# A two-group layer on one core: where the third group's second feed-forward product stands

## The chip, the cores and the metric

One core of a Trainium2 chip runs the kernel. The metric is the device time of one execution in microseconds (us), of which lower is better. The engines are TensorE (PE: matmuls; PEld: its weight loads), VectorE (DVE), ScalarE (ACT), GpSimd (POOL) and SyncE (SP), which issues most DMAs. Each engine executes its own instructions in a fixed order.

## The reference, cut to what matters

```python
u  = x*(1+sc1) + sh1                       # z = u @ w_in; then RG-LRU branch A and band attention B
x1 = LN(alpha*x + (1+g1) * ((sigmoid(ga)*A + sigmoid(gb)*B) @ w_out))
u2 = x1*(1+sc2) + sh2
y  = LN(alpha*x1 + (1+g2) * (relu(u2 @ w_up + b_up)**2 @ w_down + b_down))
```

The model width is 1024, the hidden width of the last line 4096, and there are 1024 prompt and 64 sample tokens. All is float32. The change concerns the last line only.

## The kernel before, in words

Tokens lie along the free dimension in three groups of 384, 384 and 320 (the third holds the 64 sample tokens). Every fp32 product is made of three matmuls, `mm3` (lines 108 to 111): each operand is split into a rounded high part (ScalarE, a copy, line 96 or 102) and the remainder as low part (VectorE, a subtraction, line 97 or 103).

**The up product** (`u2 @ w_up`) has 32 feature blocks, taken as 16 pairs p = 0 to 15. For pairs 3 to 15 the groups 1 and 2 together go through a seven-product scheme (`strassen`, from the weight sums that `wops` forms on GpSimd, and operands T1 to T4): accumulators `xu`, `zu`, `yu`, 12 matmuls to a product, the results `c` passed through relu and square (lines 608, 609) and written to DRAM (`hs_d`, seven operands for each of four chunks c). The third group goes through a plain product `up_g2` (accumulators `ug`, results `cg`, DRAM `hg_d`), 24 matmuls to a block. For pairs below `LATE` = 11 it stands inside its pair; for pairs 11 to 15 it comes after all pairs, from weights that are loaded and split a second time.

**The down product** follows in three steps: for each of four chunks seven operands `op` are loaded from `hs_d` and split (`op_split`; two raw buffers `opr`, seven split ones `oph`/`opl`), then four seven-product blocks (`xd`, `zd`, `yd`) are added into `facc` by VectorE (line 840). Then the third group's product `dg` runs in 2 x 4 x 4 blocks of 24 matmuls (half r of the output, chunk, output block b), for which `hg` is loaded in 16 pieces, and between these blocks `final(g, i)` normalizes the six finished token tiles of groups 1 and 2 (transposes `yt` on TensorE, statistics and a product on VectorE, an addition on GpSimd at line 872, copies on ScalarE). The last three tiles, `final(2)`, are the tail.

Before the up product, `early(i)` puts up products of pairs 0 and 1 between the steps of the first normalization (`ln1`), whose transposes `nt` give the operands `u2h`, `u2l`. The order of the instructions on each engine is set by a scheduler in the framework, which simulates the program; the order of the source is its input, `issue_after` its constraint. Weights go through three raw buffers `wraw` and three of each split part.

Of the kernel before, what the change touches and what calls it, by code (L numbers as in the profile page):

```python
# [48 lines left out]
def body(nc, tc, a):  # L49
    V, S, G, TE, SY = nc.vector, nc.scalar, nc.gpsimd, nc.tensor, nc.sync  # L50
    with ExitStack() as es:
# [552 lines left out]
        def up_w(f):  # L604
            return wsplit(a["w_up"][f], f"u{f}")
# [32 lines left out]
        def fblocks(p):  # L638
            c, i = divmod(p, 4)
            return 8 * c + i, 8 * c + 4 + i  # L640
# [11 lines left out]
        def early(i):  # L652
            for f in (ef[0:2], (), ef[2:4], ())[i] if i < 4 else ():
                wt[f] = up_w(f)
                up_mm(f, wt[f], 0)
            for f in ((), ef[0:2], (), ef[2:4])[i] if i < 4 else ():
                up_mm(f, wt[f], 1)

        ln1(2, rTs[2], early)
# [48 lines left out]
        def wops(src1, src2, nm, full):  # L708

            raw = []  # L710
            for b, src in enumerate((src1, src2)):
                r = wp.tile([P, NB, P], F32, tag="wraw", name=f"wr_{nm}{b}")
                SY.dma_start(r, src)
                raw.append(r)
            ra, rb = raw
            sr, sums = [], []
            for b in range(2):
                sr.append(spool[0].tile([P, NB, P], F32, tag="sraw", bufs=2, name=f"sr_{nm}{b}"))
                sums.append([spool[0].tile([P, NB, P], R32, tag=t, bufs=2, name=f"{t}_{nm}{b}") for t in ("shi", "slo")])
            h = slice(0, 4), slice(4, 8)  # L720
            s1, s2, s3, s4 = sr[0][:, h[1], :], sr[0][:, h[0], :], sr[1][:, h[0], :], sr[1][:, h[1], :]
            wa = [wp.tile([P, NB, P], R32, tag=t, name=f"{t}_{nm}0") for t in ("whi", "wlo")]
            split(*wa, ra)
            G.tensor_tensor(s1, rb[:, h[0], :], rb[:, h[1], :], op=ALU.add)
            G.tensor_tensor(s2, s1, ra[:, h[0], :], op=ALU.subtract)
            split(*sums[0], sr[0])
            G.tensor_tensor(s3, ra[:, h[0], :], rb[:, h[0], :], op=ALU.subtract)
            G.tensor_tensor(s4, ra[:, h[1], :], s2, op=ALU.subtract)
            split(*sums[1], sr[1])
            wb = [wp.tile([P, NB, P], R32, tag=t, name=f"{t}_{nm}1") for t in ("whi", "wlo")]  # L730
            if full:
                split(*wb, rb)
            else:
                split(wb[0][:, h[1], :], wb[1][:, h[1], :], rb[:, h[1], :])

            def half(t, k):
                return t[0][:, h[k], :], t[1][:, h[k], :]

            ops = [half(wa, 0), half(wa, 1), half(sums[0], 0), half(sums[0], 1), half(sums[1], 0), half(sums[1], 1), half(wb, 1)]
            return ops, wa, wb  # L740
# [13 lines left out]
        def up_g2(p, wa, wb):  # L754
            for b, (wt, f) in enumerate(zip((wa, wb), fblocks(p))):
                ps = acc(f"ug{p}_{b}")
                for kb in range(NB):
                    mm3(ps[:, :TW2], wt[0][:, kb, :], wt[1][:, kb, :], u2h[2][:, kb, :], u2l[2][:, kb, :], kb == 0, kb == NB - 1)
                c = fp.tile([P, TW2], F32, tag="cg", bufs=2, name=f"cg{p}_{b}")
                relu2(c, ps[:, :TW2], f)  # L760
                put_g2(p, b, c)

        PLAIN, LATE = 3, 11

        def up_pair(p):
            f1, f2 = fblocks(p)
# [36 lines left out]

        for p in range(2, 16):
            up_pair(p)
        for p in range(LATE, 16):
            up_g2(p, *(up_w(f) for f in fblocks(p)))
        up_es.close()


# [5 lines left out]
        def op_split(src, nm):  # L816
            hl = [hp.tile(list(src.shape), R32, tag=t, bufs=7, name=f"{t}{nm}") for t in ("oph", "opl")]
            split(*hl, src)
            return hl

        for c in range(4):
            ops = []
            for k in range(7):
                o = hp.tile([P, 4, GW], F32, tag="opr", bufs=2, name=f"op{c}_{k}")
                last = SY.dma_start(o, hs_d[c, k]).ins
                ops.append(op_split(o, f"{c}_{k}"))
            if c == 0:
                with tc.issue_after(last):
                    for fb in range(NB):
                        facc[fb] = hp.tile([P, TS2], F32, tag=f"facc{fb}", name=f"facc{fb}")  # L830
                        SY.dma_start(facc[fb], facc_d[:, fb, 0:TS2])
            for j in range(4):
                w, wa, wb = wops(a["w_down"][c, 2 * j], a["w_down"][c, 2 * j + 1], f"d{c}_{j}", False)

                def after(k, ps):

                    for b, g in {0: [(0, 0)], 1: [(0, 0)], 2: [(0, 1)], 3: [(1, 1)], 4: [(1, 1)], 5: [(0, 1)], 6: [(1, 0)]}[k]:
                        fb = 2 * j + b
                        fc = facc[fb][:, GW * g:GW * g + GW]
                        V.scalar_tensor_tensor(fc, ps, ada[:, G2, fb, 0:1], fc, op0=ALU.mult, op1=ALU.add)  # L840

                strassen(w, ops, f"d{c}_{j}", after)

        with tc.issue_after(last):
            fg = actb.tile([P, NB, TW2], F32, tag="act", bufs=2, name="fg")
            SY.dma_start(fg, facc_d[:, :, TS2:T])
            lgb = actb.tile([P, 2, D], F32, tag="act", bufs=2, name="lgb")
            lg, lb = lgb[:, 0, :], lgb[:, 1, :]
            SY.dma_start(lg, a["ln2"][0].partition_broadcast(P))
            SY.dma_start(lb, a["ln2"][1].partition_broadcast(P))  # L850
        hg = {}

        def facc_of(g, fb, c, cw):
            return fg[:, fb, c:c + cw] if g == 2 else facc[fb][:, GW * g + c:GW * g + c + cw]
# [32 lines left out]
            for c in todo:  # L887
                finish(*c)

        for r in range(2):  # L890
            ps = [acc(f"dg{4 * r + b}") for b in range(4)]
            for c in range(4):
                for h in range(2):
                    o = hp.tile([P, 4, TW2], F32, tag="opr", bufs=2, name=f"hg{r}_{c}_{h}")
                    SY.dma_start(o, hg_d[:, 8 * c + 4 * h:8 * c + 4 * h + 4, :])
                    hg[h] = op_split(o, f"g{r}_{c}_{h}")
                for b in range(4):
                    wh, wl = wsplit(a["w_down"][c, 4 * r + b], f"dg{r}_{c}_{b}")
                    for k in range(8):
                        o = hg[k // 4]  # L900
                        mm3(ps[b][:, :TW2], wh[:, k, :], wl[:, k, :], o[0][:, k % 4, :], o[1][:, k % 4, :],
                            c == 0 and k == 0, c == 3 and k == 7)
                if 4 * r + c < 6:
                    final((4 * r + c) // 3, (4 * r + c) % 3)
            for b in range(4):
                fb = 4 * r + b
                for c0, c1, w in parts(2):
                    fc = fg[:, fb, c0:c1]
                    V.scalar_tensor_tensor(fc, ps[b][:, c0:c1], ada[:, G2, fb, w:w + 1], fc, op0=ALU.mult, op1=ALU.add)
        final(2)  # L910


# [64 lines left out]
```

## Time and profile before

| | |
|---|---|
| three runs | 1798.82, 1793.41, 1798.59 us (median 1798.59) |
| profiled execution | 1800.96 us, its span 1798.8 us |
| TensorE busy | 1725.9 us (96%) |
| VectorE, ScalarE, GpSimd busy | 1032.6, 785.9, 452.6 us |
| mean granted clock of TensorE | 0.979 |
| moved by DMA | 228.59 MB, 127 GB/s over the span |

The profile shows one execution. A busy TensorE may still be slow, since its clock can be granted in full or in half; the mean clock of 0.979 says that about 4% of the span ran at half. Where TensorE waits, the timeline gives the length of the idle time in brackets and the instruction that ended it.

### The profile page before, as it was taken

How to read it: one execution, taken by the hardware profiler on the slowest of the kernel's cores; microseconds unless marked ns; L12 is line 12 of the kernel's file. 1: busy time of each engine (PE TensorE's matmuls, PEld its weight loads, DVE VectorE, ACT ScalarE, POOL GpSimd, SP SyncE). 2: the span in 40 equal slices, each digit the busy share in tenths (PEclk: the TensorE clock that was granted, in tenths of full speed). 3: DMA queues.
4: the chain of work that ended last, by engine and by line, in shares of the span. 5: the costliest groups of instructions: out<-in, count | busy, mean ns of one | idle time of the engine just before them, and what ended most of it. 6: DMA issues, size and time to landing. Idle time of an engine off the chain costs nothing.

```text
span 1798.8 us, 26842 instructions
## 1 busy us (share of the span) xinstructions
PE 1725.9 (96%) x10684; PEld 1687.4 (94%) x10684; DVE 1032.6 (57%) x1594; ACT 785.9 (44%) x1172; POOL 452.6 (25%) x487
## 2 busy tenths in 40 slices
PE   7999999999999999999999888999989599999996
PEld 4999999999999999999999888999989599999996
DVE  4594553737445374553656558333333568887775
ACT  2452533526244262533534445555545433443652
POOL 1100010000001000010025574556552344432111
PEclk8999999999999999999999998999989699999998
DMA  9231312112231222212255442333436644554762
GB/s 359 90 128 55 99 55 96 64 61 91 68 99 44 73 73 67 96 55 87 69 192 163 146 137 93 123 130 129 143 135 206 240 151 142 192 194 171 270 220 77
DMA packets 90269, 228.59 MB, mean 127 GB/s; under 512 B 11744, under 2 KB 42720, under 8 KB 90144
## 3 DMA queue, kind: packets, MB, share of 16 engines
q1 hardware_dynamic: 74528, 199.60, 33.1%
q10 hardware_dynamic: 11520, 14.69, 2.3%
q0 software_dynamic: 4096, 12.59, 1.9%
q8 instruction: 84, 1.38, 0.3%
q14 instruction: 41, 0.34, 0.1%
HBM read 182.01 MB, written 44.83 MB: 126 GB/s over the span
## 4 chain that ended last, share of the span: by engine, by line
PE 85%; DVE 5%; DMA 4%; issue 2%; ACT 2%; POOL 2%; SPq 0%; ACTq 0%; DVEq 0%; POOLq 0%
PE z L110 12%; PE z L111 12%; PE z L109 12%; PE po L402 3%; PE s L391 2%; PE xu L109 2%; PE dg L109 2%; PE dg L110 2%; PE dg L111 2%; PE xu L110 2%; PE xu L111 2%; DMA op<-hs_d 2%; PE xd L109 2%; PE ug L109 2%; PE ug L110 2%
## 5 line engine op out<-in xcount | busy, mean ns | idle before, releaser
L109 PE MATMUL z<-uh,wh_in 128*128 128x384 f32 (+1 forms) x1320 | 435.3, 330 | 3.1 <-ACT uh L102 3.1
L110 PE MATMUL z<-ul,wh_in 128*128 128x384 f32 (+1 forms) x1320 | 436.9, 331 | 0.2 <-DVE ul L103 0.2
L111 PE MATMUL z<-uh,wl_in 128*128 128x384 f32 (+1 forms) x1320 | 435.7, 330 | 0.0
L109 PEld LDWEIGHTS z<-uh,wh_in 128*128 128x128 f32 x1320 | 248.7, 188 | 6.4 <-ACT uh L102 4.0
L110 PEld LDWEIGHTS z<-ul,wh_in 128*128 128x128 f32 x1320 | 248.6, 188 | 4.2 <-DVE ul L103 2.2
L111 PEld LDWEIGHTS z<-uh,wl_in 128*128 128x128 f32 x1320 | 248.6, 188 | 4.0 <-issue 3.1
L96 ACT ACTIVATE wh_in<-wr_in 128x1024 fp32r<-128x1024 f32 x56 | 59.3, 1060 | 105.4 <-PE z L110 100.4
L97 DVE TENSOR_TENSOR wl_in<-wr_in,wh_in 128x1024 fp32r<-128x1024 f32 x56 | 68.5, 1223 | 43.3 <-ACT wh_in L96 43.1
L160 DVE SCALAR_TENSOR_TENSOR ap<-ar,sil,ap 128x512 f32<-128x512 f32 x112 | 79.9, 746 | 0.0
L109 PE MATMUL dg<-ophg,wh_dg 128*128 128x320 f32 x256 | 79.6, 311 | 0.0
L110 PE MATMUL dg<-oplg,wh_dg 128*128 128x320 f32 x256 | 79.1, 309 | 0.0
L111 PE MATMUL dg<-ophg,wl_dg 128*128 128x320 f32 x256 | 79.1, 309 | 0.0
L451 POOL MEMSET er<- 128x1 f32 x8 | 1.1, 136 | 296.8 <-DVE rt L447 296.8
L103 DVE TENSOR_TENSOR opl<-op,oph 128x1536 fp32r<-128x1536 f32 x28 | 60.8, 2172 | 18.9 <-ACT oph L102 18.7
L374 ACT ACTIVATE pr<-pr,st 128x640 f32<-128x640 f32 (+2 forms) x64 | 44.7, 698 | 57.7 <-DVE st L373 57.5
L102 ACT ACTIVATE shi_d<-sr_d 128x1024 fp32r<-128x1024 f32 x32 | 33.8, 1057 | 76.0 <-PE yd L110 53.1
L357 DVE COPY v<-vt 128x512 f32<-128x512 f32 x16 | 11.1, 692 | 96.9 <-PE vt L356 96.9
L103 DVE TENSOR_TENSOR slo_u<-sr_u,shi_u 128x1024 fp32r<-128x1024 f32 x26 | 32.9, 1266 | 58.6 <-ACT shi_u L102 58.6
L103 DVE TENSOR_TENSOR wlo_u<-wr_u,whi_u 128x1024 fp32r<-128x1024 f32 (+1 forms) x26 | 38.1, 1465 | 48.1 <-ACT whi_u L102 48.1
L398 ACT ACTIVATE pts<-pt 128x512 f32<-128x512 f32 (+2 forms) x64 | 33.2, 518 | 74.3 <-PE pt L396 73.2
L402 PE MATMUL po<-pts,v 128*128 128x128 f32 x480 | 64.1, 275 | 0.5 <-ACT pts L398 0.3
L330 POOL TENSOR_TENSOR ko<-kh,kl 128x512 f32<-128x512 f32 x8 | 10.3, 1292 | 212.2 <-DVE kl L324 181.8
(372 smaller groups left out, 4747.7 us busy)
## 6 DMA issues: line engine op xcount, KB each, us to landing
wr_in<-in_w_in SPq DMA_DIRECT2D x56, 512.0 KB, 3.3
ar<-in_w_ada SPq DMA_DIRECT2D x46, 512.0 KB, 5.2
wr_u<-in_w_up SPq DMA_DIRECT2D x43, 512.0 KB, 3.8
op<-hs_d SPq DMA_DIRECT2D x28, 768.0 KB, 5.0
wr_d<-in_w_down SPq DMA_DIRECT2D x32, 512.0 KB, 3.8
wr_dg<-in_w_down SPq DMA_DIRECT2D x32, 512.0 KB, 4.3
wr_o<-in_w_out SPq DMA_DIRECT2D x24, 512.0 KB, 3.4
hs_d<-t POOLq DMA_DIRECT2D x64, 192.0 KB, 2.6
```

The costliest lines, as they stand in the source:

```text
L96: S.activation(hi, raw, AF.Copy)
L97: V.tensor_tensor(lo, raw, hi.bitcast(F32), op=ALU.subtract)
L102: S.activation(hi, src, AF.Copy)
L103: V.tensor_tensor(lo, src, hi.bitcast(F32), op=ALU.subtract)
L109: TE.matmul(ps, wh, xh, start=first, stop=False, skip_group_check=more)
L110: TE.matmul(ps, wh, xl, start=False, stop=False, skip_group_check=more)
L111: TE.matmul(ps, wl, xh, start=False, stop=last, skip_group_check=more)
L160: V.scalar_tensor_tensor(part[:, w, :], raw[:, j, :], sil[:, kb, w:w + 1], part[:, w, :], op0=ALU.mult, op1=ALU.add)
L374: S.activation(pr[:rows, :W], pr[:rows, :W], AF.Exp, bias=st[:rows, 0:1], scale=-1.0, accum_out=st[:rows, 1:2])
L391: TE.matmul(sps[:, bk, :cw], qq[:, q0:q0 + P], kk[:, P * j0 + c0:P * j0 + c0 + cw], start=(ip == 0), stop=(ip == 2))
L398: S.activation(pts[:, :min(W, 512)], pt[:, :min(W, 512)], AF.Copy)
L402: TE.matmul(po[:, :P], v[:, j0 + j, :], pts[:, P * j:P * j + P], start=(j == 0), stop=(j == nk - 1))
```

## The change

1. `early`: the last of the four up products of group 2 is put behind the last step of the first normalization.
2. `LATE` becomes 14: pairs 11 to 13 keep their third-group product inside the pair; only those of pairs 14 and 15 come late, with 4 weight blocks loaded again and not 10.
3. The third group's down product is cut in two. The half over chunks 0 and 1 stands between the up product and the seven-product down stage (from here on: the first half), the half over chunks 2 and 3 at the end (the second half). `hg` is loaded once, in 8 pieces; VectorE adds the accumulators to `fg` twice.
4. The loads of `hg` for chunk 0 are issued between the late weights of pair 14 and those of pair 15 (`issue_after`). The loads of `facc` are spread behind operand loads, `fg` and `lgb` (the normalization's parameters) are loaded earlier.
5. The six `final` tiles come after every second block of the second half.

```diff
-            for f in ((), ef[0:2], (), ef[2:4])[i] if i < 4 else ():
+            for f in ((), ef[0:2], (), ef[2:3], ef[3:4])[i]:
                 up_mm(f, wt[f], 1)
...
-        PLAIN, LATE = 3, 11
+        PLAIN, LATE = 3, 14
...
-        for p in range(LATE, 16):
-            up_g2(p, *(up_w(f) for f in fblocks(p)))
         up_es.close()
...
+        def load_hg(c, h):
+            o = hp.tile([P, 4, TW2], F32, tag="opr", bufs=2, name=f"hg{c}_{h}")
+            loads.append(SY.dma_start(o, hg_d[:, 8 * c + 4 * h:8 * c + 4 * h + 4, :]).ins)
+            return op_split(o, f"g{c}_{h}")
+
+        def down_g2(cs, hg, after):
+            for r in range(2):
+                ps = [acc(f"dg{4 * r + b}_{cs[0]}") for b in range(4)]
+                for c in cs:
+                    for b in range(4):
+                        wh, wl = wsplit(a["w_down"][c, 4 * r + b], f"dg{r}_{c}_{b}")
+                        for k in range(8):
+                            o = hg[c, k // 4]
+                            mm3(ps[b][:, :TW2], wh[:, k, :], wl[:, k, :], o[0][:, k % 4, :], o[1][:, k % 4, :],
+                                c == cs[0] and k == 0, c == cs[-1] and k == 7)
+                        after()
...
+        loads = []
+        wt = [up_w(f) for f in fblocks(LATE)]
+        hg = {(0, h): load_hg(0, h) for h in range(2)}
+        up_g2(LATE, *wt)
+        with tc.issue_after(loads[-1]):
+            for p in range(LATE + 1, 16):
+                up_g2(p, *(up_w(f) for f in fblocks(p)))
+        hg.update({(1, h): load_hg(1, h) for h in range(2)})
+        fg = actb.tile([P, NB, TW2], F32, tag="act", bufs=2, name="fg")
+        SY.dma_start(fg, facc_d[:, :, TS2:T])
+        down_g2((0, 1), hg, lambda: None)
...
             for j in range(4):
+                if c == 0:
+                    with tc.issue_after(loads[4 + (0, 4, 6, 6)[j]]):
+                        for fb in (2 * j, 2 * j + 1):
+                            facc[fb] = hp.tile([P, TS2], F32, tag=f"facc{fb}", name=f"facc{fb}")
+                            SY.dma_start(facc[fb], facc_d[:, fb, 0:TS2])
...
-                if 4 * r + c < 6:
-                    final((4 * r + c) // 3, (4 * r + c) % 3)
...
+        hg = {(c, h): load_hg(c, h) for c in (2, 3) for h in range(2)}
+        fin = iter([(g, i) for g in range(2) for i in range(3)])
+
+        def next_final():
+            step[0] += 1
+            if step[0] % 2 == 0 and step[0] <= 12:
+                final(*next(fin))
+
+        step = [0]
+        down_g2((2, 3), hg, next_final)
         final(2)
```

**TensorE, end of the first normalization.** `up5_1` is the product that part 1 of the change moves, `nt2_256` the last transposes of the normalization. Before:

```order
L110 MATMUL up5_1_9715<-u2l1_8934,wh_u5_9606 128x384
L111 MATMUL up5_1_9715<-u2h1_8933,wl_u5_9607 128x384
L572 MATMUL nt2_256_9742<-ident_72,n12_256_9655 128x64 x8
L109 MATMUL up5_2_9773<-u2h2_9377,wh_u5_9606 128x320
L109 MATMUL up1_2_9800<-u2h2_9377,wh_u1_9572 128x320
```

With the change:

```order
L110 MATMUL up5_1_9746<-u2l1_8934,wh_u5_9606 128x384
L111 MATMUL up5_1_9746<-u2h1_8933,wl_u5_9607 128x384
L572 MATMUL nt2_256_9715<-ident_72,n12_256_9655 128x64 x8
L109 MATMUL up5_2_9773<-u2h2_9377,wh_u5_9606 128x320
L109 MATMUL up1_2_9800<-u2h2_9377,wh_u1_9572 128x320
```

Only the numbers of the accumulators differ: the scheduler puts the transposes behind the product as before.

**SyncE, from the last pair's weights on.** Before, all late weights stand ahead of the first operand load `op0_0`:

```order
L92 DMA wr_u27_12815<-in_w_up 128x1024
L92 DMA wr_u31_12821<-in_w_up 128x1024
L713 DMA wr_d0_00_12952<-in_w_down 128x1024
L713 DMA wr_d0_01_12954<-in_w_down 128x1024
L713 DMA wr_d0_10_13072<-in_w_down 128x1024
L825 DMA op0_0_12894<-hs_d_88 128x1536
L825 DMA op0_1_12900<-hs_d_88 128x1536
```

With the change (`wr_u26`, `wr_u30` belong to pair 14, `wr_u27`, `wr_u31` to pair 15, `wr_dg` to the first half):

```order
L92 DMA wr_u30_12724<-in_w_up 128x1024
L821 DMA hg0_0_12730<-hg_d_89 128x1280
L821 DMA hg0_1_12736<-hg_d_89 128x1280
L92 DMA wr_u27_12800<-in_w_up 128x1024
L92 DMA wr_u31_12806<-in_w_up 128x1024
L92 DMA wr_dg0_0_0_12888<-in_w_down 128x1024
L821 DMA hg1_0_12870<-hg_d_89 128x1280
L821 DMA hg1_1_12876<-hg_d_89 128x1280
L92 DMA wr_dg0_0_1_12918<-in_w_down 128x1024
```

The two `hg` loads now stand ahead of pair 15's weights, and further down operand loads of the seven-product stage stand among the first half's weights:

```order
L858 DMA op0_0_13388<-hs_d_88 128x1536
L865 DMA facc0_13430<-facc_d_87 128x768
L865 DMA facc1_13432<-facc_d_87 128x768
L858 DMA op0_1_13394<-hs_d_88 128x1536
L92 DMA wr_dg0_1_0_13008<-in_w_down 128x1024
L851 DMA fg_12882<-facc_d_87 128x8x320
L879 DMA lgb_15492<-in_ln2 128x1024
L880 DMA lgb_15492<-in_ln2 128x1024
L92 DMA wr_dg0_1_1_13038<-in_w_down 128x1024
```

Before, these operands, `facc`, `fg` and `lgb` shared the queue with no `wr_dg`.

**ScalarE, the conversion of the last late weights** (`wh_u27`, `wh_u31`). Before:

```order
L608 ACTIVATE cg13_0_12712<-ug13_0_12687,bup_78 128x320
L609 ACTIVATE cg13_0_12712<-cg13_0_12712 128x320
L636 DMA hg_d_89<-cg13_0_12712 128x320
L96 ACTIVATE wh_u27_12817<-wr_u27_12815 128x1024
L608 ACTIVATE cg13_1_12741<-ug13_1_12716,bup_78 128x320
```

With the change:

```order
L608 ACTIVATE cg14_0_12767<-ug14_0_12742,bup_78 128x320
L608 ACTIVATE cg14_1_12796<-ug14_1_12771,bup_78 128x320
L609 ACTIVATE cg14_0_12767<-cg14_0_12767 128x320
L609 ACTIVATE cg14_1_12796<-cg14_1_12796 128x320
L636 DMA hg_d_89<-cg14_0_12767 128x320
L636 DMA hg_d_89<-cg14_1_12796 128x320
L102 ACTIVATE ophg0_0_12732<-hg0_0_12730 128x1280
L102 ACTIVATE ophg0_1_12738<-hg0_1_12736 128x1280
L96 ACTIVATE wh_u27_12802<-wr_u27_12800 128x1024
L96 ACTIVATE wh_u31_12808<-wr_u31_12806 128x1024
```

The high part of pair 15's first weights, `wh_u27`, stands behind the relu of `ug14_1` and behind both `ophg` splits; before, they were converted two products ahead, between the results of pair 13, and no operand split stood ahead of them.

## Rows read from the trace of the kernel before

**Rows 1.** the page: span, and chain that ended last by engine

```profile
span 1798.8 us, 26842 instructions
...
PE 85%; DVE 5%; DMA 4%; issue 2%; ACT 2%; POOL 2%; SPq 0%; ACTq 0%; DVEq 0%; POOLq 0%
```

**Rows 2.** waits of TensorE, two of the longest (total us, times, longest)

```profile
PE xd L109 <- DVE facc L840: 7.5, 3, 5.9
PE up L109 <- ACT u2h L102: 6.3, 2, 4.9
```

**Rows 3.** 20 us stretches: busy PE, PEld, DVE, ACT, POOL; clock, DMA share, GB/s

```profile
1280.00:1300.00 20.00, 20.00 (x117) 20.00 (x117) 8.81 (x9) 9.90 (x16) 10.79 (x12) 1.00 0.41 128
...
1400.00:1420.00 20.00, 9.73 (x27) 8.06 (x28) 11.28 (x7) 8.52 (x7) 15.15 (x8) 0.55 0.43 146
1420.00:1440.00 20.00, 14.12 (x67) 13.80 (x66) 12.33 (x13) 6.58 (x5) 0.86 (x1) 0.77 0.91 357
1600.00:1620.00 20.00, 18.53 (x104) 17.56 (x104) 17.39 (x16) 10.25 (x9) 7.48 (x4) 1.00 0.81 286
1660.00:1680.00 20.00, 20.00 (x135) 19.99 (x134) 15.20 (x14) 11.97 (x12) 0.00 (x0) 1.00 0.75 245
```

**Rows 4.** timeline of TensorE, unfilled pairs (start, us, operation, [idle before, its end])

```profile
1302.69 0.34 PE L111 MATMUL xu<-T2h,slo_u 128*128 128x384 f32 x1
...
1339.29 0.44 PE L109 MATMUL xu<-T2h,shi_u 128*128 128x384 f32 x1 [2.55 <-ACT c L782]
...
1343.20 0.69 PE L109 MATMUL xu<-T3h,shi_u 128*128 128x384 f32 x1 [0.63 <-ACT c L787]
...
1347.21 0.38 PE L109 MATMUL yu<-u2h,shi_u 128*128 128x384 f32 x1
```

**Rows 5.** timeline of ScalarE ahead of the stall at 1339.29

```profile
1336.28 0.56 ACT L608 ACTIVATE c<-xu,bup 128x384 f32<-128x384 f32 x1
1336.74 1.05 ACT L96 ACTIVATE wh_u<-wr_u 128x1024 fp32r<-128x1024 f32 x1
...
1338.75 0.49 ACT L782 ACTIVATE c<-xu 128x384 f32<-128x384 f32 x1 [0.56 <-ACT c L609]
```

**Rows 6.** timeline of TensorE at the switch from the up to the down product

```profile
1396.95 0.31 PE L111 MATMUL ug<-u2h,wl_u 128*128 128x320 f32 x1
1401.49 0.44 PE L109 MATMUL xd<-oph,whi_d 128*128 128x384 f32 x1 [4.23 <-ACT oph L102]
...
1433.05 0.69 PE L109 MATMUL xd<-oph,shi_d 128*128 128x384 f32 x1 [5.88 <-DVE facc L840]
...
1436.61 0.35 PE L109 MATMUL yd<-oph,shi_d 128*128 128x384 f32 x1
...
1438.71 0.33 PE L109 MATMUL xd<-oph,shi_d 128*128 128x384 f32 x1
```

**Rows 7.** groups of the last stage, 1655 to 1781 (busy us, mean ns | idle before)

```profile
L97 DVE TENSOR_TENSOR wl_dg<-wr_dg,wh_dg 128x1024 fp32r<-128x1024 f32 x30 | 45.6, 1518 | 14.1 <-ACT wh_dg L96 13.9
L103 DVE TENSOR_TENSOR oplg<-hg,ophg 128x1280 fp32r<-128x1280 f32 x14 | 20.8, 1485 | 5.1 <-ACT ophg L102 5.0
L102 ACT ACTIVATE ophg<-hg 128x1280 fp32r<-128x1280 f32 x14 | 17.8, 1270 | 11.5 <-DMA hg<-hg_d 8.0 <-PE dg L111 3.4 <-PE xd L111 0.2
L872 POOL TENSOR_TENSOR y<-y,lgb 128x1024 f32<-128x1024 f32 x6 | 16.3, 2709 | 20.9 <-DVE y L871 10.9 <-issue 10.0
L518 DVE BATCH_NORM_STATS2 lstb<-y 128x6 f32<-128x512 f32 x12 | 7.7, 679 | 0.0
L871 DVE TENSOR_TENSOR y<-y,lgb 128x1024 f32<-128x1024 f32 x6 | 7.4, 1226 | 4.2 <-ACT y L869 4.2
L878 PE MATMUL yt<-ident,facc 128*128 128x128 f32 x48 | 6.2, 272 | 0.0
```

**Rows 8.** timeline of VectorE, two weight splits in the last stage

```profile
1701.54 1.22 DVE L97 TENSOR_TENSOR wl_dg<-wr_dg,wh_dg 128x1024 fp32r<-128x1024 f32 x1
1703.61 2.50 DVE L97 TENSOR_TENSOR wl_dg<-wr_dg,wh_dg 128x1024 fp32r<-128x1024 f32 x1 [0.85 <-ACT wh_dg L96]
```

More of the change, by code (lines that the diff above doesn't have):

```diff
@@ L758, in up_g2 @@
                     mm3(ps[:, :TW2], wt[0][:, kb, :], wt[1][:, kb, :], u2h[2][:, kb, :], u2l[2][:, kb, :], kb == 0, kb == NB - 1)
-                c = fp.tile([P, TW2], F32, tag="cg", bufs=2, name=f"cg{p}_{b}")
+                c = spool[0].tile([P, TW2], F32, tag="cg", bufs=2, name=f"cg{p}_{b}")
                 relu2(c, ps[:, :TW2], f)
                 put_g2(p, b, c)
-        PLAIN, LATE = 3, 11
+        PLAIN, LATE = 3, 14
         def up_pair(p):
@@ L819, in op_split @@
             return hl
+        def load_hg(c, h):
[13 more added lines that the diff above has]
+                        after()
+                for b in range(4):
+                    fb = 4 * r + b
+                    for c0, c1, w in parts(2):
+                        fc = fg[:, fb, c0:c1]
+                        V.scalar_tensor_tensor(fc, ps[b][:, c0:c1], ada[:, G2, fb, w:w + 1], fc, op0=ALU.mult, op1=ALU.add)
+        loads = []
[9 more added lines that the diff above has]
+        down_g2((0, 1), hg, lambda: None)
         for c in range(4):
@@ L824, in body @@
                 o = hp.tile([P, 4, GW], F32, tag="opr", bufs=2, name=f"op{c}_{k}")
-                last = SY.dma_start(o, hs_d[c, k]).ins
+                loads.append(SY.dma_start(o, hs_d[c, k]).ins)
                 ops.append(op_split(o, f"{c}_{k}"))
[L827 to L831, printed above, removed]
-            for j in range(4):
+            for j in range(4):
+                if c == 0:
[3 more added lines that the diff above has]
+                            SY.dma_start(facc[fb], facc_d[:, fb, 0:TS2])
                 w, wa, wb = wops(a["w_down"][c, 2 * j], a["w_down"][c, 2 * j + 1], f"d{c}_{j}", False)
@@ L842, in body @@
                 strassen(w, ops, f"d{c}_{j}", after)
[L844 to L851, printed above, removed]
+        lgb = actb.tile([P, 2, D], F32, tag="act", bufs=2, name="lgb")
+        lg, lb = lgb[:, 0, :], lgb[:, 1, :]
+        SY.dma_start(lg, a["ln2"][0].partition_broadcast(P))
+        SY.dma_start(lb, a["ln2"][1].partition_broadcast(P))
         def facc_of(g, fb, c, cw):
@@ L888, in final @@
                 finish(*c)
[L890 to L902, printed above, removed]
-                if 4 * r + c < 6:
-                    final((4 * r + c) // 3, (4 * r + c) % 3)
[L905 to L909, printed above, removed]
+        hg = {(c, h): load_hg(c, h) for c in (2, 3) for h in range(2)}
[6 more added lines that the diff above has]
+        down_g2((2, 3), hg, next_final)
         final(2)
```

## The prediction

> **What bounds the kernel now.** I read the page first. Of the chain that ended last 85% is TensorE itself, inside a span of 1798.8 us [rows 1]. The number of matmuls isn't changed, so only time in which TensorE waits, or runs at the lower granted clock, can be won. The next view is TensorE's waits, for where they are: one of 5.9 us on `facc` at the switch from the up to the down product, one of 4.9 us on `u2h` at the end of the first normalization [rows 2]. The 20 us stretches then show where the loss is dense. From 1280 to 1300, where third-group products fill the pairs, TensorE is busy for the whole 20.00 us; from 1400 to 1420 for 9.73 at a granted clock of 0.55, from 1420 to 1440 for 14.12 at 0.77; from 1660 to 1680, in the third group's down product, again for 20.00 [rows 3]. So two places matter, the unfilled pairs before 1347 and the switch.
>
> The measure is the issue rate at full clock: 12 matmuls of 384 columns from 1436.61 to 1438.71, 0.175 us each [rows 6], so 0.146 for 320 columns, and 3.5 us for a block of 24. At the lower level 12 matmuls take 4.01 us, from 1343.20 to 1347.21 [rows 4].
>
> *Unfilled pairs.* Between 1302.69 and 1347.21 lie 181 matmuls, 31.7 us of work in 44.5: 12.8 us are lost [rows 4]. It goes through ScalarE: TensorE waits 2.55 us for the copy of an accumulator, and the copy stands behind a relu and a weight conversion of 1.05 us [rows 4, 5]. After the wait come matmuls at the lower clock, and a second wait of 0.63.
>
> *The switch.* Between the last `ug` matmul (1396.95, done at 1397.10) and 1438.71 TensorE issues 84 matmuls, 14.7 us of work in 41.6: 26.9 us are lost, of which 4.23 before the first operand is split and 5.88 when `facc` isn't there [rows 6].
>
> **The change, part by part.**
>
> *The early product* (part 1): TensorE's order is the same, so its 4.9 us [rows 2] stay. 0; I see nothing on the other engines there that moves.
>
> *Pairs 11 to 13 filled.* The loss should vanish where third-group products stand between the steps, as it does from 1280 to 1300 [rows 3]. Pairs 14 and 15 remain. In the new order one wait is left, for the copy of pair 15's first accumulator behind pair 14's last relu, square and DMA issue; the conversion now stands ahead of the relu. In the old case the relu began at 1336.28 and TensorE resumed at 1339.29 [rows 4, 5]; less some 0.85 of conversion that is exposed, 2.2 us. The row that this is nearest to is the 2.55 wait, so I let the lower clock follow: as there the first twelve matmuls take 3.3 us and not 2.1 (from 1339.29 to 1343.20, less the 0.63 of waiting), then comes the wait of 0.6, and the next twelve take 4.0, 1.9 too long. Sum 2.2 + 1.2 + 0.6 + 1.9 = 5.9 left, 12.8 - 5.9 = **6.9 gained**. Ends: 9.9 if the clock stays up, 6.5 if the wait is 2.55 again. The six weight blocks no longer loaded and split were beside other work: 0.
>
> *The switch.* (a) Between `ug14_1` and `ug15_0` a new wait appears. From the end of `ug14_1` ScalarE has a relu, two squares (0.5 each, as the relu of 0.56 and copy of 0.49 [rows 5]) and two DMA issues, some 2.3 in all, then two `ophg` of 1.27 [rows 7], then `wh_u27` of 1.05 [rows 5]: TensorE's first matmul can go after 5.9. Its third needs `wl_u27`, and VectorE has two `oplg` of 1.49 ahead of it, from 3.6 on, then 1.23 itself [rows 7, 8]: 7.8, less two matmuls already done, a **7.4 us wait**. Queued behind it are all of `ug15` and the first half. After the old wait of 5.88 twelve matmuls took 3.56 instead of 2.10 [rows 6]: 1.5 more (ends 0, and 7, if all 48 of `ug15` run at half). The loads are in time: `hg0_0` is issued when pair 15's sixth product ends, 12 + 48 matmuls or 9 us before the wait starts.
> (b) The first half then covers the load of the seven operands, `facc`, `fg` and `lgb`, whose loads move from an idle stretch into a busy one. From the issue of `hg0_0` to the end of the first half are 9 + 16 + 16 x 3.5 = 81 us, in which 18 weight blocks (9.4 MB), four `hg` (2.6), seven `op` (5.5), `facc` (3.1), `fg` and `lgb` (2.4) and two blocks for the next stage (1.0) want to come: 24.1 MB, 298 GB/s. The rows show 357, 286 and 245 GB/s [rows 3]: at 357 nothing waits, at 286 it takes 84 us, 3 too many, at 245 98 us, 17 too many. At 245 TensorE was never idle, so that may be all that was asked for; the 286, where TensorE lost 1.5 of 20 us, is nearest. I take 3.
> (c) At the end of the first half `op5` and `op6` wait for split buffers which `hg` holds, but they are used only after five products of 2.1 us, and a split takes 1.27 + 1.49 [rows 7]. I take 1 (0 to 3).
> Left: 7.4 + 1.5 + 3 + 1 = 12.9; 26.9 - 12.9 = **14.0 gained** (19.5 with the wait alone; 1.5 with 7 for the clock, 8 for loads and 3).
>
> *Finals twice as dense.* Two blocks and eight transposes (48 in 6.2 [rows 7]) give TensorE 7.0 + 1.0 = 8.0 us to a final. VectorE has two statistics of 0.68, a product of 1.23 and two weight splits of 1.52 on the mean [rows 7], 5.6 us, plus short steps and the added `fg` sums; it fits, with waits for ScalarE like the 0.85 in [rows 8]. **1 lost** (0 to 5, six times 0.85). The cover here is three split buffers of weights; without it each excess goes to TensorE.
> A page of the Trainium skill speaks against this part: "SBUF — State Buffer", section "SBUF: two separate sides", says that GpSimd and a VectorE operation with two inputs hold their common ports by an exclusive lock, and that the loser is blocked for the whole instruction. The trace agrees in part: a split of 1.22 takes 2.50 beside the final's GpSimd addition [rows 8], which itself lasts 2.71 [rows 7]. By the full rule six finals would block VectorE 2.7 us each and not 1.28; that is the third rival.
>
> **Sum.** 6.9 + 14.0 - 1 = 19.9 us. Against the profiled execution's own 1800.96 that is 1781.1. The three runs' median lies 2.4 below it, so measured 1778.7; I say **1779**, with ends of its own at 1770 and 1787.
>
> **Rivals.**
> *Smaller: the hole only moves.* The 7.4 us wait is followed by the lower clock through all of `ug15` (5.5 more), and the loads cost 8 instead of 3. For it: at the old switch the clock was 0.55 over twenty microseconds [rows 3]. Against: `ug15` and the first half have no waits between them such as the old switch had. Gain 9.4, 1789. Chance 0.20.
> *Larger.* The clock stays up in the pairs (3 more), after the wait (1.5), and neither loads nor buffers hold TensorE (4). Gain 28.4, 1770. For it: 357 GB/s were moved in 1420 to 1440. Chance 0.14.
> *VectorE becomes the bound of the second half.* Each final costs 1.4 more (2.7 less 1.28), six 8.4. 1787. Against it: only one split of each final is slow. Chance 0.07.
> *Slower: the first half is starved.* SyncE's queue is in order, and a load that waits for its buffer (two for operands, three for weights) holds those behind it: `op0_0`, two `facc`, `op0_1` stand ahead of `wr_dg0_1_0`, `fg` and `lgb` ahead of `wr_dg0_1_1`. Where operand loads were handed over one by one, 146 GB/s were moved [rows 3]. At 216, the middle between that and 286, the 24.1 MB take 112 us, 31 more than the 81 there are: instead of 3 lost 31, so 1807. It turns slower than before at some 23 us of starving, 24.1 MB in 104 us or 232 GB/s. Against: weights and operands have buffers of their own, and 286 was moved with both. Chance 0.09.
> The Trainium skill has a rule that leans to this rival: "DMA: Bandwidth & Descriptors", section "Queues, rings and completion order", says that on each DMA engine descriptors are consumed in the order of the ring, so a weight block would come only after all that was queued ahead of it.
> *That an edit does nothing*: so it stands with the early product, in the order itself; it is in the sum.
>
> **How the numbers follow.** The forecast has the other 0.50. A measurement of this kernel can tell about 0.3%, 5.4 us, from no change. Faster: the first three rivals and the forecast give 0.91, of which the tails (much worse ends together) take 0.05: 0.86. Slower: two thirds of the last rival and a little of the tails, 0.07; the rest, 0.07, is no change. The range runs from below the larger gain to above the smaller one, 1767 to 1791, and leaves out the starved case and half of the tails.
>
> **What would show it.** Right: TensorE's stretches before the switch busy for 20.00 except one wait near 2.2 us; a single wait of 7 to 8 us on `wh_u`/`wl_u` between two `ug` products; small waits for `wr_dg` in the first half, with about 300 GB/s; no 5.9 us wait on `facc`; the 4.9 us wait on `u2h` as before. Wrong: waits of `dg` on weights in the first half of more than 10 us in all, a granted clock near half there, or `dg` waiting on `wl_dg` between finals in the second half.

## The result and the profile after

The changed kernel takes 1780.7 us in the median of 4 runs (1777.1 to 1782.16), against 1798.7 (1793.41 to 1804.3) before: a ratio of 0.9897, 95% interval 0.9863 to 0.9930. That is 18.0 us by the medians; the profiled executions, 1800.96 and 1780.97 us, differ by 20.0.

| | before | after |
|---|---|---|
| median of 4 runs, us | 1798.7 | 1780.7 |
| profiled execution, its span, us | 1800.96, 1798.8 | 1780.97, 1779.0 |
| mean granted clock | 0.979 | 0.984 |
| TensorE busy | 1725.9 us (96%) | 1718.8 us (97%) |
| moved by DMA | 228.59 MB | 220.20 MB |

The page of the changed kernel, the chain by engine, as in [rows 1]:

```profile
PE 86%; DVE 5%; issue 3%; DMA 2%; ACT 2%; POOL 1%; SPq 0%; ACTq 0%; DVEq 0%; POOLq 0%
```

TensorE has 86% of the chain where it had 85%. The number of matmuls is the same in both traces (10684). Of the 19.8 us by which the span is shorter, 12.7 are TensorE's waits and 7.1 its busy time, shorter for as many matmuls, since fewer of them run at the lower clock.

TensorE's waits in the changed kernel (total us, times, longest), to be read against [rows 2]:

```profile
PE up L109 <- ACT u2h L102: 6.3, 2, 4.9
PE ug L109 <- ACT wh_u L96: 5.3, 1, 5.3
...
PE xu L109 <- ACT c L782: 4.9, 2, 3.0
PE xd L111 <- DVE wlo_d L103: 3.6, 3, 2.0
...
PE xd L109 <- DVE facc L873: 2.5, 3, 0.9
PE dg L111 <- DVE wl_dg L97: 1.6, 1, 1.6
```

The long wait on `facc` is gone (0.9 at most). The wait on `u2h` is what it was. New are the 5.3 on `wh_u` between two late products, 1.6 of `dg` on a weight block, and 2.0 on `wlo_d` at the start of the seven-product stage.

The 20 us stretches of the changed kernel, with the columns of [rows 3] (busy PE, PEld, DVE, ACT, POOL; clock, DMA share, GB/s):

```profile
1360.00:1380.00 20.00, 16.33 (x82) 15.77 (x82) 3.11 (x4) 8.40 (x15) 9.29 (x13) 0.83 0.48 163
1380.00:1400.00 20.00, 13.66 (x73) 13.00 (x72) 10.51 (x8) 11.91 (x15) 1.37 (x3) 0.74 0.88 321
1400.00:1420.00 20.00, 18.39 (x125) 18.13 (x124) 10.22 (x9) 9.40 (x10) 0.00 (x0) 1.00 0.99 382
1420.00:1440.00 20.00, 20.00 (x139) 20.00 (x138) 10.37 (x14) 6.80 (x7) 0.00 (x0) 1.00 0.75 264
...
1720.00:1740.00 20.00, 20.00 (x144) 19.98 (x143) 17.57 (x24) 11.20 (x15) 5.92 (x4) 1.00 0.62 196
```

From 1120 to 1360 the pairs run without a gap (20.00 us in each stretch, not shown). The loss is in 1360 to 1400. In the first half, TensorE loses 1.6 us from 1400 to 1420, while 382 GB/s are moved, and nothing after it until its end; 2.0 us more are lost behind it, at 1468. In the second half, with a final after every second block, it loses nothing.

TensorE's timeline from the last pair to the seven-product stage, the places of [rows 4] and [rows 6] in the changed kernel:

```profile
1363.10 0.44 PE L109 MATMUL xu<-T2h,shi_u 128*128 128x384 f32 x1 [3.04 <-ACT c L782]
...
1366.94 0.69 PE L109 MATMUL xu<-T3h,shi_u 128*128 128x384 f32 x1 [0.63 <-ACT c L787]
...
1370.94 0.45 PE L109 MATMUL yu<-u2h,shi_u 128*128 128x384 f32 x1
```

```profile
1387.69 0.63 PE L109 MATMUL ug<-u2h,wh_u 128*128 128x320 f32 x1 [5.28 <-ACT wh_u L96]
...
1389.65 0.64 PE L111 MATMUL ug<-u2h,wl_u 128*128 128x320 f32 x1 [1.06 <-DVE wl_u L97]
...
1398.92 0.31 PE L109 MATMUL dg<-ophg,wh_dg 128*128 128x320 f32 x1
```

The wait for the accumulator's copy is 3.04 us, and of the 24 matmuls from 1363.10 on all but the first six are slow (the granted clock from 1366 to 1371 is 0.50): the first twelve take 3.84 less the second wait of 0.63, the next twelve 4.00, instead of 2.10 each. Between the late products of pairs 14 and 15 TensorE stands for 5.28 us, issues two matmuls, stands for 1.06, and takes 9.27 us for the next 46, where 0.146 each would be 6.7.

ScalarE ahead of that wait:

```profile
1382.45 0.53 ACT L608 ACTIVATE cg<-ug,bup 128x320 f32<-128x320 f32 x1 [2.99 <-PE ug L111]
1382.88 0.82 ACT L609 ACTIVATE cg<-cg 128x320 f32<-128x320 f32 x2
1383.36 0.85 ACTq L636 DMA_DIRECT2D hg_d<-cg  x2
1384.26 2.43 ACT L102 ACTIVATE ophg<-hg 128x1280 fp32r<-128x1280 f32 x2 [0.57 <-ACT cg L609]
1386.60 1.99 ACT L96 ACTIVATE wh_u<-wr_u 128x1024 fp32r<-128x1024 f32 x2
```

This is the predicted chain, name by name: relu, two squares, two DMA issues, two `ophg`, then `wh_u`. The raw weight blocks were there before: their loads were issued at 1374.25 and 1374.8 and landed 6.8 and 8.7 us later, so by 1383.5, and the conversion began at 1386.60.

### The profile page after: what moved, and what is told of

Same layout as the page of the kernel before. It is cut to its first block, busy times and chain, and to the rows that moved or that the text cites. A ratio compares the mean times of both kernels' runs of the same rounds, so it can differ in the third digit from the quotient of the medians.

```text
span 1779.0 us, 26773 instructions
## 1 busy us (share of the span) xinstructions
PE 1718.8 (97%) x10684; PEld 1682.1 (95%) x10684; DVE 1012.8 (57%) x1596; ACT 771.4 (43%) x1158; POOL 457.4 (26%) x487
## 2 busy tenths in 40 slices
DMA packets 88253, 220.20 MB, mean 124 GB/s; under 512 B 11520, under 2 KB 42496, under 8 KB 88128
## 4 chain that ended last, share of the span: by engine, by line
PE 86%; DVE 5%; issue 3%; DMA 2%; ACT 2%; POOL 1%; SPq 0%; ACTq 0%; DVEq 0%; POOLq 0%
PE z L111 12%; PE z L110 12%; PE z L109 12%; PE po L402 3%; PE s L391 2%; PE xu L109 2%; PE xu L110 2%; PE xu L111 2%; PE dg L111 2%; PE dg L109 2%; PE dg L110 2%; PE xd L109 2%; PE ug L111 2%; PE xd L111 2%; PE ug L109 2%
```

## The experiments

All were timed in 4 to 6 runs each beside runs of the kernel before. Ratios are to the kernel before, with 95% intervals.

**1. Without the filling.** Is it the filled pairs or the switch that pays?

```diff
-        PLAIN, LATE = 3, 14
+        PLAIN, LATE = 3, 11
```

> The changed kernel with LATE back at 11: pairs 11 to 13 lose their third-group filling again. My theory (the filling pays for part of the gain, 12.8 us lost there before and 6.7 us in the changed kernel): two waits of about 2.5 to 3 us on the copy of an accumulator come back in the pairs, time 6 us above the changed kernel, some 1787 us, the rest of the gain (13 us) stays. Rival (all of the gain comes from the switch, filling is only moved work): no change against 1780.7 us. Second rival (late products are needed to cover the hg loads, and more of them make the switch cheaper): below 1780 us.

Measured: 1788.86 us (ratio 0.9935, 0.9918 to 0.9951), 8.2 above the changed kernel. TensorE's four longest kinds of wait from 1295 to 1480:

```profile
PE xu L109 <- ACT c L782: 8.1, 3, 3.0
PE ug L109 <- ACT wh_u L96: 5.3, 1, 5.3
PE yu L109 <- ACT shi_u L102: 2.1, 2, 1.0
PE xu L109 <- ACT c L787: 1.3, 2, 0.6
```

The waits in the pairs are 11.5 us (8.1, 2.1 and 1.3), where the changed kernel has 3.7 (3.04 and 0.63); the new wait at the late products stays at 5.3. So the first theory holds. More late products did not shorten that wait; the two smaller ones behind it did shrink (0.69 for 1.61 on `wl_dg`, 0.42 for 2.02 on `wlo_d`).

**2. The filling alone.**

```diff
 (kernel before)
-        PLAIN, LATE = 3, 11
+        PLAIN, LATE = 3, 14
```

> The kernel before with LATE at 14 and nothing else: the down product is not split. The order on TensorE puts the late products of pairs 14 and 15 between the products of pair 15, so my theory expects nearly no wait in the pairs: 12 us gained there, and the switch unchanged at 27 us lost: 1787 us (1784 to 1790). Rival (the six loads and splits that fall away matter, beside the filling): below 1783 us. Rival (with fewer late products ahead of the switch its hole grows by what the pairs give back): 1795 to 1800 us and a hole over 35 us.

Measured: 1787.47 us (0.9934, 0.9916 to 0.9951), 12.0 below the kernel before. Two of its stretches, and its two longest kinds of wait from 1295 to 1480:

```profile
1340.00:1360.00 20.00, 20.00 (x120) 20.00 (x119) 7.36 (x8) 10.15 (x16) 8.49 (x12) 1.00 0.44 147
1380.00:1400.00 20.00, 8.92 (x24) 7.33 (x24) 11.38 (x7) 8.99 (x10) 16.51 (x13) 0.66 0.52 181
```

```profile
PE xd L109 <- DVE facc L840: 6.8, 2, 6.2
PE xd L109 <- ACT oph L102: 3.8, 1, 3.8
```

No wait is left in the pairs, and the hole at the switch is as large as before (waits of 3.8, 1.1, 3.7, 1.9, 1.9 and 6.2 us between 1380 and 1416). It didn't grow, so the second rival falls; and the time is not below 1783 us, so no gain of the loads that fall away can be told from the filling's.
Filling alone brings 12.0, the rest of the change alone 10.6 (1799.46 less 1788.86), the two together 18.0. The 4.6 between them is not shown by the times, whose intervals are 3 us to each side for the two experiments and 6 for the change. The traces show what would make it: here the late products stand between the products of pair 15, while in the change they come after them, and pair 15 waits 3.04 and 0.63 us, with the slow matmuls behind.

**3. Pair 15's weights ahead of hg.**

```diff
-        hg = {(0, h): load_hg(0, h) for h in range(2)}
         up_g2(LATE, *wt)
-        with tc.issue_after(loads[-1]):
-            for p in range(LATE + 1, 16):
-                up_g2(p, *(up_w(f) for f in fblocks(p)))
+        for p in range(LATE + 1, 16):
+            wt = [up_w(f) for f in fblocks(p)]
+            if p == 15:
+                hg = {(0, h): load_hg(0, h) for h in range(2)}
+            up_g2(p, *wt)
```

> The changed kernel without the constraint that queues the hg loads ahead of pair 15's weights: SyncE issues both weight blocks of pair 15 and three of the first half before the first hg. My theory (the 6.3 us wait between the late products and the half clock behind it, 8.9 us in all, come from ScalarE having the hg splits and the results of pair 14 ahead of pair 15's weights): that wait goes, one of 1 to 3 us appears before the first dg block, 6 us gained, some 1775 us. Rival (loads of hg first are what keeps the first half fed): a wait of 6 us or more before or in the first half, 1781 us or above.

Measured: 1773.71 us (0.9853, 0.9832 to 0.9873), 7.0 below the changed kernel. TensorE at the first block of the first half, and at the start of the seven-product stage:

```profile
1386.73 0.56 PE L109 MATMUL dg<-ophg,wh_dg 128*128 128x320 f32 x2 [0.27 <-ACT ophg L102]
```

```profile
1454.75 0.69 PE L109 MATMUL xd<-oph,shi_d 128*128 128x384 f32 x1 [5.80 <-ACT shi_d L102]
```

The wait of 6.3 us between the late products is gone, and 0.8 us is left at the first block (0.27, and 0.38 and 0.17 right after). So the first step of part 4 of the change, `hg` loads queued ahead of pair 15's weights, cost more than it brought. What none of the theories had is the 5.80 at the end: the weights of the first seven-product block were issued at 1437.90 behind two `op` and four `facc` and took 9.6 us to land, and GpSimd's sums for `shi_d` started only then.

**4. A quarter instead of a half ahead of the stage.**

```diff
-        hg.update({(1, h): load_hg(1, h) for h in range(2)})
...
-        down_g2((0, 1), hg, lambda: None)
+        down_g2((0,), hg, lambda: None)
...
-                    with tc.issue_after(loads[4 + (0, 4, 6, 6)[j]]):
+                    with tc.issue_after(loads[2 + (0, 4, 6, 6)[j]]):
...
-        hg = {(c, h): load_hg(c, h) for c in (2, 3) for h in range(2)}
+        hg = {(c, h): load_hg(c, h) for c in (1, 2, 3) for h in range(2)}
...
-        down_g2((2, 3), hg, next_final)
+        down_g2((1, 2, 3), hg, next_final)
```

> Only chunk 0 of the third group's down product ahead of the seven-product stage, chunks 1 to 3 behind it. My theory (the first half covers the loads: 24.1 MB in 81 us): now 18.6 MB have 53 us, 351 GB/s, at 321 to 382 GB/s 0 to 5 us too many, and the last operands come later: 3 to 8 us above the changed kernel, 1784 to 1789 us, with waits at the start of the seven-product stage. Rival (any work between the two stages will do, the size does not matter): 1781 us, no more waits than in the changed kernel.

Measured: 1783.16 us (0.9904, 0.9888 to 0.9920), 2.5 above the changed kernel, less than was expected and not to be told from the changed kernel. The stretch with its operand loads:

```profile
1400.00:1420.00 20.00, 17.68 (x110) 16.77 (x109) 14.48 (x17) 11.30 (x11) 0.00 (x0) 0.92 1.01 380
```

It moves 380 GB/s there, 336 in the next 20 us, and TensorE has four small waits from 1415 to 1445 (1.13, 0.44, 0.75 and 0.99). So the budget of 81 us for the loads was not tight: with 53 us, by the expectation's count, nothing is lost that can be told from the noise, and the size of the first half is no reason for the gain by itself.

**5. The moved up product really behind the transposes.**

```diff
+                nt_last[0] = TE.transpose(...)
...
-            for f in ((), ef[0:2], (), ef[2:3], ef[3:4])[i]:
+            for f in ((), ef[0:2], (), ef[2:3])[i] if i < 4 else ():
                 up_mm(f, wt[f], 1)
+            if i == 4:
+                with tc.issue_after(nt_last[0].ins):
+                    up_mm(ef[3], wt[ef[3]], 1)
```

> The changed kernel with a constraint that really puts the moved up product behind the last transposes of the first normalization, which part 1 of the change did not do. My theory (the chain from the normalized tile to u2h lasts 5.6 us and now starts 24 matmuls earlier, as soon as the tile is there): the 4.9 us wait on u2h becomes one of 2 to 3 us ahead of the transposes and one below 1 us, 1 to 3 us gained, 1778 to 1780 us. Rival (the tile is not there any earlier, so the wait only moves ahead of the transposes): still 4.9 us in all, 1781 us.

Measured: 1774.47 us (0.9862, 0.9844 to 0.9879), 6.2 below the changed kernel by the medians. The transposes in its timeline:

```profile
1043.43 0.98 PE L574 MATMUL nt<-ident,n 64*128 64x64 f32 x8 [1.92 <-ACT n L564]
```

There is one wait of 1.92 us and none on `u2h` behind it any more. From the transposes before these to a place with the same 448 matmuls behind it, some 80 us on, it is 81.6 us (1036.28 to 1117.85) where the changed kernel has 86.1 (1038.39 to 1124.45): 4.5 us are shown in the trace. Of these 3.0 are the wait (1.92 for 4.87); the rest falls at the first seven-product pair, where the waits come in another order. That the medians say 6.2 may be spread between programs: this execution was already 2.1 us ahead before the edited place. The direction is clear, the size is 3 to 6.

**6. The normalization's parameters out of the first half.**

```diff
+        with tc.issue_after(loads[-1]):
             SY.dma_start(lg, a["ln2"][0].partition_broadcast(P))
             SY.dma_start(lb, a["ln2"][1].partition_broadcast(P))
```

> The changed kernel with the two loads of the normalization's parameters (1 MB) put behind the last operand load, out of the first half. My theory (the first half is within a few us of being starved, and its one wait of 1.6 us on a weight block comes from these loads standing ahead of that block): the 1.6 us wait goes, 1.6 us gained, about 1779 us. Rival (the wait comes from the rate at which buffers come free): it stays, 1781 us.

Measured: 1779.2 us (0.9895, 0.9879 to 0.9912). The stretch in which `dg` waited:

```profile
1400.00:1420.00 20.00, 20.00 (x138) 19.98 (x137) 11.54 (x11) 10.37 (x11) 0.00 (x0) 1.00 0.92 351
```

TensorE is busy for 20.00 of 20 us there, where it was for 18.39: the 1.6 us wait is gone. At the start of the seven-product stage the wait on `wlo_d` is 0.53 instead of 2.02 us; that one is 0.56 in experiment 5 and 1.86 in 7, where no load was moved, so it isn't put to this edit. The 1.5 us by which the median falls are too few to be told from no change in the time itself; the trace shows the wait of 1.6 gone.

**7. A final after every block.**

```diff
-            if step[0] % 2 == 0 and step[0] <= 12:
+            if 2 <= step[0] <= 7:
```

> The changed kernel with the six finals after the second to the seventh block of the second half, one after each block instead of every second. My theory (VectorE needs about 5 us to a final and a block, TensorE 4.5, three buffers of weights ahead): 0 to 4 us lost, 1781 to 1785 us. Rival (VectorE and GpSimd exclude each other for the whole of each addition): 1.4 us more to each final, over 8 us lost, 1789 us or above. Second rival (VectorE has room to spare): no wait at all, 1781 us.

Measured: 1780.82 us (0.9897, 0.9880 to 0.9914), the same as the changed kernel. Its densest stretch and the next, and VectorE's product in a final, by line from 1690 to 1761:

```profile
1720.00:1740.00 20.00, 20.00 (x140) 19.73 (x139) 19.38 (x28) 11.59 (x17) 10.68 (x6) 1.00 0.49 171
1740.00:1760.00 20.00, 19.06 (x131) 18.80 (x130) 14.02 (x14) 6.59 (x8) 5.66 (x2) 1.00 0.44 156
```

```profile
L900 DVE TENSOR_TENSOR y<-y,lgb 128x1024 f32<-128x1024 f32 x6 | 11.7, 1943 | 1.1 <-ACT y L898 1.1
```

VectorE is busy for 19.38 of 20 us and its product takes 1.94 us on the mean instead of 1.23 in the changed kernel, and still TensorE waits 0.9 us only (the stretch after it). The rival's price is out by this: it asked for 8 us. Whether an addition blocks VectorE is another question, and the rows answer it (under *Finals* below).

**8. The findings together.** Experiments 3, 5 and 6, the load of `fg` behind the last `hg`, and `facc` 2 to 7 each behind the weights of the block before the one that uses them:

```diff
                 r = wp.tile(...)
-                SY.dma_start(r, src)
+                wlast[0] = SY.dma_start(r, src).ins
...
-                    with tc.issue_after(loads[4 + (0, 4, 6, 6)[j]]):
+                    with tc.issue_after(wlast[0] if j else loads[4]):
```

> Weights of pair 15 ahead of the hg loads, parameters of the normalization behind the last operand load, the load of fg behind the last hg, those of facc 2 to 7 each behind the weights of the seven-product block before it, and the transposes ahead of the moved up product. Where the version with pair 15's weights first still had a 5.8 us wait at the start of the seven-product stage (its weights landed 9.6 us after their issue, behind four facc and two operand loads) there should be at most 1 us: 1774 less 5, less 1 for its clock, less 1 to 3 for the transposes: 1766 us. Rival (the loads only crowd another place): a wait of 3 us or more on facc or operands, 1771 us or above.

Measured: 1763.91 us (0.9801, 0.9783 to 0.9818): below the interval of the change (0.9863 at its lower end). Its longest waits from 1300 to 1480:

```profile
PE xu L109 <- ACT c L789: 3.0, 1, 3.0
PE xd L111 <- DVE wlo_d L103: 1.1, 1, 1.1
```

The 5.8 is gone; at the start of the seven-product stage 1.1 is left, on another operand. What remains is the last pair. The expected 1766 us is met, and the rival's wait of 3 us or more on `facc` or operands isn't there. What the edits to `fg` and `facc` bring each by itself was not tried.

**9. One late product only.** As 8 with `LATE` = 15, the first `hg` behind pair 15's weights and split ahead of its results:

```diff
-        PLAIN, LATE = 3, 14
+        PLAIN, LATE = 3, 15
...
+        hg = {(0, h): load_hg(0, h) for h in range(2)}
+        with tc.issue_after(last_act[0]):
+            up_g2(LATE, *wt)
...
+        with tc.issue_after(loads[1]):
+            down_g2((0, 1), hg, lambda: None)
```

> As the version before (weights first, loads spread, transposes ahead), but LATE at 15: pair 14 keeps its third-group product inside, only that of pair 15 comes late; the first two hg stand behind pair 15's weights and ahead of the first half's, and ScalarE splits them ahead of pair 15's results. My theory (a pair that is filled has no wait): of the 3.0 and 0.6 us waits in the last pairs and the lower clock behind them, about 6 us, most go, but one late product covers the hg loads for 9 us only, so 2 to 3 us come back before the first dg block: 1758 to 1762 us against 1763.9. Rival (one late product is too short a cover): a wait of 6 us or more ahead of dg, 1764 us or above.

Measured: 1763.32 us (0.9796, 0.9782 to 0.9809), the same as 8; expected was 2 to 6 less. Its waits from 1300 to 1420:

```profile
PE dg L111 <- ACT wh_dg L96: 2.4, 2, 1.6
PE dg L113 <- DVE wl_dg L97: 1.4, 2, 0.7
PE xu L111 <- ACT c L796: 0.6, 1, 0.6
```

The 3.04 is gone and 3.8 us of waits on the first half's weights have come; the expectation had put 2 to 3 us there, for the shorter cover. The trade is even. Neither theory's number was met.

**10. The copy ahead of the conversion.** Why the wait in the last pair was 3.04 us and not the 2.2 of the forecast:

```diff
                 if k == 0:
-                    S.activation(c11, ps, AF.Copy)
+                    copy[0] = S.activation(c11, ps, AF.Copy).ins
...
-        wt = [up_w(f) for f in fblocks(LATE)]
+        with tc.issue_after(copy[0]):
+            wt = [up_w(f) for f in fblocks(LATE)]
```

> The changed kernel with the conversions of pair 14's late weights put behind the copy for which TensorE waits 3.04 us in pair 15. My theory (one conversion of 1.06 us, which itself waits for a buffer, stands ahead of the relu and the copy): the wait falls to 2.0 to 2.4 us, 0.7 to 1 us gained, and up to 3 us more if the clock stays up behind the shorter wait: 1776 to 1780 us. Rival (relu, square and DMA issue alone make the wait): it stays at 3 us, 1781 us.

Measured: 1777.76 us (0.9885, 0.9868 to 0.9902), 2.9 less by the medians, inside the interval of the change. TensorE there:

```profile
1361.48 0.44 PE L109 MATMUL xu<-T2h,shi_u 128*128 128x384 f32 x1 [2.28 <-ACT c L783]
...
1365.41 0.44 PE L109 MATMUL xu<-T3h,shi_u 128*128 128x384 f32 x1 [1.55 <-ACT c L788]
```

The first wait is 2.28 us, the rival falls. The second grows from 0.63 to 1.55, because both conversions now stand ahead of the results of the pair. The clock stayed up (1.00 from 1360 to 1370): from 1361.48 to 1365.41, less 1.55, twelve matmuls take 2.4 us.

**11. The same in the version of 8.**

> The version at 1763.9 us (weights first, loads spread, transposes ahead) with the same edit: its 3.04 us wait falls to 2.0 to 2.4, 1 to 4 us gained, 1760 to 1763 us. Rival: the conversions come late and the first late product waits for them instead, 1764 us.

Measured: 1762.41 us (0.9795, 0.9778 to 0.9811), the lowest, but not to be told from 8 and 9. Its waits in the pair are 2.27 and 0.63, and there is no new one at the late products.

## Why the prediction was right

The forecast was 1779 us, the gain 19.9 against the profiled execution; measured were 1780.7, between its own ends of 1770 and 1787, and 20.0. The mechanism came as forecast in the pairs and at the late products; that the sum is met within 1 us is in part luck, as terms that were too small and too large offset each other. The terms, by the prediction's own steps:

| step | predicted | shown by the trace of the change |
|---|---|---|
| early product | 0 | 4.87 us wait on `u2h` in both |
| pairs: left of 12.8 lost | 5.9 | 3.04 + 1.1 + 0.63 + 1.9 = 6.7 |
| switch (a): wait, slow matmuls | 7.4 + 1.5 | 5.28 + 1.06 = 6.3, and 2.5 |
| switch (b): loads | 3 | 1.6 |
| switch (c): split buffers | 1 | 0 (no wait of TensorE on `oph` or `opl`) |
| not forecast: `wlo_d` | 0 | 2.0 |
| finals | 1 | 0 |
| gain | 19.9 | 12.8 - 6.7 + 26.9 - 12.4 = 20.6; 20.0 measured |

*The early product.* Reading the order decided this: the source was moved and the order was not. Experiment 5 shows what the edit would have been worth, 3 us or more.

*Pairs.* Experiments 1 and 2 show that the filling works as the argument from a filled stretch said. The mis-sized term is the wait itself, 2.2 predicted and 3.04 measured, in the step "the conversion now stands ahead of the relu": it does, but it waits for a buffer until the matmuls before it have ended. ScalarE in the changed kernel:

```profile
1359.91 1.06 ACT L96 ACTIVATE wh_u<-wr_u 128x1024 fp32r<-128x1024 f32 x1 [1.69 <-PE xu L110]
1360.88 0.56 ACT L608 ACTIVATE c<-xu,bup 128x384 f32<-128x384 f32 x1
...
1362.55 0.49 ACT L782 ACTIVATE c<-xu 128x384 f32<-128x384 f32 x1 [0.56 <-ACT c L609]
```

The conversion starts at 1359.91, after 1.69 us of waiting for TensorE, so most of its 1.06 us stands ahead of the relu and TensorE waits for it. From the relu's start to TensorE's next matmul it is 2.22 us (1360.88 to 1363.10), the 2.2 of the forecast; with the conversion out of the way (experiment 10) the wait itself is 2.28.

*The switch.* The new wait was found in the order of ScalarE's rows and priced from durations: 7.4 predicted, 6.3 measured; the two squares and the two DMA issues overlap (1382.88 to 1384.26 instead of 1.7 us one after another). That this order causes it was shown by experiment 3. The slow matmuls behind it were under-priced by 1.0, the loads over-priced by 1.4.

The over-pricing of the loads comes from a row that was read wrongly. The prediction took the 1.5 us that TensorE lost from 1600 to 1620 as the price of moving 286 GB/s. In the trace of the kernel before, these are two waits for VectorE, and none for a load:

```profile
1611.39 0.44 PE L111 MATMUL xd<-oph,wlo_d 128*128 128x384 f32 x1 [0.76 <-DVE wlo_d L103]
1616.39 0.44 PE L109 MATMUL xd<-oph,shi_d 128*128 128x384 f32 x1 [0.70 <-DVE facc L840]
```

The loads' one wait comes from the place that the prediction named for the starved case: the two parameter loads ahead of a weight block. ScalarE stands for 6.51 us there:

```profile
1413.98 1.06 ACT L96 ACTIVATE wh_dg<-wr_dg 128x1024 fp32r<-128x1024 f32 x1 [6.51 <-DMA wr_dg<-in_w_down]
```

Here the rule of the Trainium skill that was set beside this rival ("DMA: Bandwidth & Descriptors", section "Queues, rings and completion order", on descriptors consumed in the order of the ring) fits: with the loads ahead taken away, `dg` doesn't wait (experiment 6). The rival itself was wrong in size, since 382 GB/s were moved where it assumed 216.

What the argument had too strictly is the budget in (b): experiment 4 cuts the cover to 53 us and loses at most a few us.

The step (c) came to nothing: no product waits for `op5` or `op6`. The 2.0 us on `wlo_d` have another cause, which the prediction didn't have. VectorE is busy without a gap from 1457.69 on, and a split that takes 1.22 us elsewhere takes 2.28 beside one of GpSimd's weight sums, which ends at 1467.18:

```profile
1465.98 2.28 DVE L103 TENSOR_TENSOR wlo_d<-wr_d,whi_d 128x1024 fp32r<-128x1024 f32 x1
```

That this makes the wait is read from the rows and was not tried; it differs from run to run (0.56 us in experiment 5, 1.86 in 7).

*Finals.* Even twice as dense as in the change (experiment 7) they cost TensorE 0.9 us. The prediction said that the trace agrees with the rule of the Trainium skill only in part ("SBUF — State Buffer", section "SBUF: two separate sides"). The rows agree with it in full. In the changed kernel an addition of GpSimd ends at 1725.19, and the split that began beside it ends 1.09 us later:

```profile
1722.78 2.41 POOL L901 TENSOR_TENSOR y<-y,lgb 128x1024 f32<-128x1024 f32 x1 [3.15 <-DVE y L900]
1723.21 3.07 DVE L97 TENSOR_TENSOR wl_dg<-wr_dg,wh_dg 128x1024 fp32r<-128x1024 f32 x1
```

It is the same 1.08 or 1.09 us behind the other two additions that a split met, and behind the one of [rows 8], whose addition ran until 1705.02. Where the split came first, the addition was held instead (3.27 and 3.28 us for 2.41). So the later one waits for the rest of the earlier one. The three splits became 1.5 to 1.9 us longer by it, not by the 2.7 of a whole addition, which was the rival's price. That TensorE doesn't wait for it because of the three buffers of weights ahead is argued, not tried.

*The rivals.* The hole did not just move: 12.4 of 26.9 us are left. The larger gain did not come, since the two waits remained. But it can be had: the prediction's 1770 is passed by the version of experiment 8, at 1764.

## What to carry to other kernels

Read the order that the scheduler made, not the source: one part of this change did nothing, and another put 6 us of waiting on TensorE that no line of the source shows. When loads are queued ahead of others, look at the engine that converts them, too: here the converting engine's order, and not the arrival of the data, was the price. And check after moving work whether it still stands where it filled a gap; two edits that bring 12.0 and 10.6 us alone brought 18.0 together, and in the traces the one took the filling of the other's last gap (that this is the whole of the difference is within the noise, not shown).

## What the runs showed of the hardware

The clock behind the same wait differed. In the changed kernel, of the 24 matmuls behind the 3.04 us wait in the last pair, the first six ran at full speed and the rest slow, the second twelve at half (4.00 us, above; granted clock 0.50). In the version of experiment 3 the same wait of 3.04 us, at the same place of the same work, was followed by full speed:

```profile
1362.85 0.45 PE L109 MATMUL xu<-T2h,shi_u 128*128 128x384 f32 x1 [3.04 <-ACT c L782]
...
1365.86 0.44 PE L109 MATMUL xu<-T3h,shi_u 128*128 128x384 f32 x1 [0.63 <-ACT c L787]
...
1368.07 0.33 PE L109 MATMUL yu<-u2h,shi_u 128*128 128x384 f32 x1
```

The first twelve matmuls take 3.01 us less the 0.63 of waiting, the next twelve 2.21, against 2.10 in an unbroken run; the granted clock from 1360 to 1375 is 1.00. In experiment 1 the first twelve took 3.8 us without the wait and the second 2.2. So a wait of this length cost between 0.4 and 3.0 us beside itself in these runs, and a forecast can only give both ends. What decides between them was not tried.

The core's DMA moved 382 GB/s over 20 us in the changed kernel (share 0.99) and 401 in experiment 9, where the most that the trace of before had in the stretches read was 357:

```profile
1380.00:1400.00 20.00, 16.23 (x95) 15.17 (x95) 11.53 (x10) 11.40 (x12) 0.00 (x0) 0.92 1.03 401
```
